# A transformer trunk on one core: two tiles of the constant pool change places, and one empty tile is put before three others

## The chip, the cores and the metric

The kernel runs on one core of one Trainium2 chip. The metric is the device time of one execution in microseconds. A core has TensorE (PE in the profile; PEld is its weight load), VectorE (DVE), ScalarE (ACT), GpSimd (POOL) and SyncE (SP, which here issues the loads). SBUF, the working memory, has 128 partitions; a tile takes the same byte range in all of them, and "offset" below means the byte within a partition at which a tile starts.

## The reference

Two layers act on 256 latent tokens and 256 context tokens of width 1024. Each layer is a half SwiGLU feed-forward, a mixer, and another half feed-forward, all modulated by a conditioning vector. The mixer of layer 0 joins bidirectional mLSTM heads and a spatial gating unit; that of layer 1 is windowed attention with rotary positions.

```python
def _modulate(h, shift, scale):
    return _rms_norm(h) * (1.0 + scale) + shift

def _swiglu(h, w_in, w_out):
    g, u = jnp.split(h @ w_in, 2, axis=-1)
    return (jax.nn.silu(g) * u) @ w_out

    for layer in range(DEPTH):
        ...
        h = h + 0.5 * mod[:, 2] * _swiglu(_modulate(h, mod[:, 0], mod[:, 1]),
                                          ffn_w_in[layer, 0], ffn_w_out[layer, 0])
        ...
        h = h + mod[:, 5] * yx
        h = h + 0.5 * mod[:, 8] * _swiglu(_modulate(h, mod[:, 6], mod[:, 7]),
                                          ffn_w_in[layer, 1], ffn_w_out[layer, 1])
    return _rms_norm(h) * final_norm
```

D_MODEL is 1024 and D_FF 2816. The context stream runs through the same layers with its own modulation vector.

## The kernel before

Activations are kept transposed: 128 features on the partitions, 8 tiles of features (kt), and 512 columns, which are the 256 context and the 256 latent tokens side by side. H is the residual stream, 8 x 512 numbers of 4 bytes per partition. The normalised and modulated activation is split into a high part NH (in the format fp32r) and a remainder NL, so that the activation is the sum of both. Weights come from memory as 1 MB tiles (raw, rawx, loaded by SP at L212), and each is split in the same way into wh (ACT, L259) and wl (DVE, L243). One product of activation and weight is then three matmuls into one PSUM bank, in the function mm3:

```python
        self.M.matmul(ps, lhsT=wh, rhs=xh, start=start, stop=False)
        self.M.matmul(ps, lhsT=wh, rhs=xl, start=False, stop=False)
        self.M.matmul(ps, lhsT=wl, rhs=xh, start=False, stop=stop)
```

These are lines 415, 416 and 417. The operand called rhs is the moving one: it is streamed through the array, 512 columns of 4 bytes for a whole tile. lhsT is the stationary one: 128 columns of a weight tile, 512 bytes per partition, loaded by a weight load before its matmul. A unit is one weight block of 128 output features; it runs mm3 for its 8 kt (6 in the last part of a down projection).

- In the up projections of a feed-forward block the moving operands are NH and NL, and wh and wl are stationary. Their results go through silu and a product into hd, which is split into HH and HL.
- In the down projections HH and HL move.
- The first four units of a block are run together by `start` and `steps` (L444) or by `split_start` (L710, in halves of 256 columns), so that the first features can be used before the last are made.
- In the mixer of layer 0 some projections are token-major (L1124 to L1126): there wh and wl move, 512 columns wide, and NH and NL are stationary. At its end the gated result is turned into the tiles Fh, Fu and Fl, which move in the output projection together with the first half of NH.
- In the last feed-forward block only the latent half is computed: NH and NL then move 258 columns, HH and HL 256.

Instructions stand in the order in which the program writes them, engine by engine. Tiles live in pools; a pool gives its tiles places one after the other in the order of first use. The pool cp (constants, made in `setup`) comes first, then the ring of raw, wh and wl, then temporaries, then pools that are opened and closed for each block. The tiles NL0 to NL7 belong to cp, behind all that `setup` makes. The pool ef, opened inside `even`, holds F.

The places in the built program, by their offset modulo 2048 (all kt slices of one tile have the same, a slice of 512 columns being 2048 bytes):

| tile | before | changed kernel |
|---|---|---|
| H, NH | 2016 | 1408 |
| NL0 to NL7 | 1408 | 1408 |
| wh, wl, raw | 1408 | 1408 |
| HH, HL | 384 | 384 |
| SS, AX, SC | 2016 | 2016 |
| Fh, Fu, Fl | 864 | 1408 |

Of the kernel before, what the change touches and what calls it, by code (L numbers as in the profile page):

```python
# [9 lines left out]
F32 = mybir.dt.float32  # L10
F32R = mybir.dt.float32r
# [9 lines left out]
KT = 8  # L21
# [125 lines left out]
class Trunk:  # L147
# [312 lines left out]
    def setup(self):  # L460
        nc, a, V, S = self.nc, self.a, self.V, self.S
        cp = self.cp
        self.SM = cp.tile([128, S_N], F32, name="SM")
        self.C = cp.tile([128, C_N], F32, name="C")
        self.H = cp.tile([128, KT, 512], F32, name="H")
        self.NH = cp.tile([128, KT, 512], F32R, tag="NH", name="NH")
        self.X = [[self.NH[:, k] for k in range(KT)], [None] * KT]
        self.A = [None] * KT
        self.SS = cp.tile([128, 512], F32, name="SS")
        self.AX = cp.tile([128, KT, 256], F32, name="AX")  # L470
        self.SC = cp.tile([128, KT, 32], F32, name="SC")
        self.ONE = cp.tile([128, 128], F32, name="ONE")
        self.NHF = cp.tile([128, 4], F32, name="NHF")
        self.IDB = cp.tile([128, 128], BF16, name="IDB")
        self.MKB = cp.tile([128, 2, 128], BF16, name="MKB")
        mods = cp.tile([128, 18, KT, 2], F32, name="mods")
        self.MOD = {(l, j): mods[:, 9 * l + j] for l in range(2) for j in range(9)}
        nc.sync.dma_start(self.SM, a["small"])
        xv = a["xt"].rearrange("(k p) t -> p k t", p=128)
        for k in range(0, KT, 2):  # L480
            nc.sync.dma_start(self.H[:, k:k + 2, :], xv[:, k:k + 2, :])
        nc.sync.dma_start(self.C, a["const"])
        self.widen("f00")
        V.memset(self.ONE, 1.0)
        V.memset(self.NHF, -0.5)
        V.memset(self.SC, 0.0)
        S.activation(self.SC[:, :, 0:2], self.SM[:, S_C:S_C + 16].rearrange("p (k s) -> p k s", s=2), AF.Silu)
        self.AB = self.SM[:, S_AB:S_AB + 144].rearrange("p (l j t) -> p l j t", l=2, j=9)
        V.tensor_scalar(self.AB[:, :, 1::3, :], self.AB[:, :, 1::3, :], 1.0, None, ALU.add)
        V.tensor_scalar(self.AB[:, :, 2::6, :], self.AB[:, :, 2::6, :], 0.5, None, ALU.mult)  # L490
        self.ID = self.C[:, C_ID:C_ID + 128]
        self.heat(HEAT[0])
        for k in range(KT):
            self.add_squares()
            self.square(k, 0, 512)
        V.tensor_copy(self.IDB, self.ID)
# [314 lines left out]
    def even(self):  # L811
# [3 lines left out]
        with self.tc.tile_pool(name="ev", bufs=1) as ep, ExitStack() as xs:  # L815
# [283 lines left out]
            def to_feature(src, t, hi, lo):  # L1099
                ps = self.bank("ptf")  # L1100
                for i in range(4):
                    M.transpose(ps[:, 128 * i:128 * i + 128], src[:, 128 * i:128 * i + 128], self.ID)
                q = slice(128 * t, 128 * t + 128)
                pv = ps.rearrange("p (k t) -> p k t", k=4)
                S.copy(hi[:, :, q], pv)
                V.tensor_tensor(lo[:, :, q], pv, hi[:, :, q].bitcast(F32), ALU.subtract)
# [66 lines left out]
            def to_u(t):  # L1173
                if not F:
                    self.drain()
                    xs.close()
                    fp = xs.enter_context(self.tc.tile_pool(name="ef", bufs=1))
                    F.extend(fp.tile([128, 4, 512], F32R, name="F" + x) for x in ("h", "u", "l"))
                to_feature(U[:, t], t, F[0], F[1])

# [3 lines left out]
            def mid(n, b, i):  # L1184
                if i == 3 and (n, b) in HAT:
                    to_h(HAT[n, b])

            self.later(*[nop] * UNOPS, *[lambda t=t: to_u(t) for t in range(4)], *[nop] * (14 - 5 - UNOPS), lambda: to_h(0))
            token_major(1536, o_evac)
            self.flush()  # L1190
# [371 lines left out]
```

## Time and profile before

| what | value |
|---|---|
| median of 3 runs | 1721.47 us (1721.23 to 1723.42) |
| the profiled execution | 1723.75 us |
| its span, first to last instruction | 1721.6 us |
| granted TensorE clock | 0.997 |
| PE busy | 1706.8 us, 9702 matmuls |
| weight loads busy | 1441.0 us |
| DVE, ACT busy | 1143.2 us, 652.8 us |
| read from memory | 245.28 MB, 143 GB/s over the span |

Busy time of PE counts a matmul from its start to its modelled end, and matmuls overlap: the mean duration in a group is longer than the time between two starts. In a row of a group, the names behind the operation are result and operands, then the stationary block (128*128), the moving shape, the count, the busy time in us, the mean of one in ns, and the idle time before with what ended it. The view by stretches gives for each stretch the busy time of each engine with the number of instructions, the granted clock and the DMA share.

### The profile page before, as it was taken

How to read it: one execution, taken by the hardware profiler on the slowest of the kernel's cores; microseconds unless marked ns; L12 is line 12 of the kernel's file. 1: busy time of each engine (PE TensorE's matmuls, PEld its weight loads, DVE VectorE, ACT ScalarE, POOL GpSimd, SP SyncE). 2: the span in 40 equal slices, each digit the busy share in tenths (PEclk: the TensorE clock that was granted, in tenths of full speed). 3: DMA queues.
4: the chain of work that ended last, by engine and by line, in shares of the span. 5: the costliest groups of instructions: out<-in, count | busy, mean ns of one | idle time of the engine just before them, and what ended most of it. 6: DMA issues, size and time to landing. Idle time of an engine off the chain costs nothing.

```text
span 1721.6 us, 23813 instructions
## 1 busy us (share of the span) xinstructions
PE 1706.8 (99%) x9702; PEld 1441.0 (84%) x9702; DVE 1143.2 (66%) x1997; ACT 652.8 (38%) x1083; POOL 24.7 (1%) x29
## 2 busy tenths in 40 slices
PE   8999999999999999999999999999999999999998
PEld 6778778779888898787787898787788897799998
DVE  5876776777877857767766367646554477576665
ACT  3422232225545444222222253222212357654444
POOL 0000000000000100000000000000000000000000
PEclk9999999999999999999999999999999999999999
DMA  9654454441211234435544134444533031165540
GB/s 352 235 179 147 171 194 144 169 153 44 98 50 49 101 121 178 185 128 193 196 147 146 38 140 183 165 161 171 196 147 123 25 123 58 50 239 188 186 156 29
DMA packets 36462, 247.87 MB, mean 144 GB/s; under 512 B 4000, under 2 KB 4256, under 8 KB 8960
## 3 DMA queue, kind: packets, MB, share of 16 engines
q1 hardware_dynamic: 35792, 244.57, 39.0%
q8 instruction: 76, 1.25, 0.3%
q0 software_dynamic: 272, 1.25, 0.2%
q10 hardware_dynamic: 288, 0.52, 0.1%
q14 instruction: 34, 0.28, 0.0%
HBM read 245.28 MB, written 1.05 MB: 143 GB/s over the span
## 4 chain that ended last, share of the span: by engine, by line
PE 96%; DVE 2%; ACT 1%; DMA 0%; issue 0%; SPq 0%; POOLq 0%; ACTq 0%; DVEq 0%
PE bank L415 25%; PE bank L417 25%; PE bank L416 25%; PE bank L710 5%; PE bank L444 4%; PE bank L1126 1%; PE bank L1125 1%; PE bank L1124 1%; PE pva L337 1%; PE pov L1314 1%; PE psc L1278 1%; PE ppt L1299 1%; PE pada L383 0%; DMA H<-xt 0%; PE pO L1006 0%; PE pB L1008 0%
## 5 line engine op out<-in xcount | busy, mean ns | idle before, releaser
L415 PE MATMUL bank<-NH,wh 128*128 128x512 f32 (+2 forms) x1416 | 519.0, 367 | 0.0
L417 PE MATMUL bank<-NH,wl 128*128 128x512 f32 (+2 forms) x1416 | 514.5, 363 | 1.2 <-DVE wl L243 1.2
L416 PE MATMUL bank<-NL,wh 128*128 128x512 f32 (+2 forms) x1384 | 499.1, 361 | 0.0
L415 PEld LDWEIGHTS bank<-NH,wh 128*128 128x128 f32 x1416 | 266.1, 188 | 48.7 <-issue 9.0
L417 PEld LDWEIGHTS bank<-NH,wl 128*128 128x128 f32 x1416 | 265.9, 188 | 47.1 <-DVE wl L243 1.7
L416 PEld LDWEIGHTS bank<-NL,wh 128*128 128x128 f32 x1384 | 260.3, 188 | 45.1
L259 ACT CAST wh<-raw 128x1024 fp32r<-128x1024 f32 (+1 forms) x207 | 212.4, 1029 | 153.6 <-PE bank L416 99.8
L415 PE MATMUL bank<-HH,wh 128*128 128x512 f32 (+1 forms) x776 | 269.8, 348 | 0.0
L416 PE MATMUL bank<-HL,wh 128*128 128x512 f32 (+1 forms) x776 | 268.4, 346 | 0.1
L417 PE MATMUL bank<-HH,wl 128*128 128x512 f32 (+1 forms) x776 | 268.4, 346 | 0.0
L243 DVE TENSOR_TENSOR wl<-raw,wh 128x1024 fp32r<-128x1024 f32 (+1 forms) x207 | 246.9, 1197 | 18.7 <-ACT wh L259 18.7
L625 DVE SCALAR_TENSOR_TENSOR H<-bank,mods,H 128x256 f32<-128x256 f32 x192 | 86.6, 480 | 174.2 <-PE bank L417 171.5
L790 ACT CAST HH<-hd 128x512 fp32r<-128x512 f32 (+1 forms) x88 | 49.9, 567 | 320.5 <-DVE hd L789 285.2
L259 ACT CAST wh<-rawx 128x1024 fp32r<-128x1024 f32 (+1 forms) x118 | 119.8, 1016 | 118.2 <-PE bank L416 102.2
L415 PEld LDWEIGHTS bank<-HH,wh 128*128 128x128 f32 x776 | 147.1, 190 | 20.3 <-issue 2.5
L416 PEld LDWEIGHTS bank<-HL,wh 128*128 128x128 f32 x776 | 147.1, 190 | 17.9 <-DVE HL L791 0.3
L417 PEld LDWEIGHTS bank<-HH,wl 128*128 128x128 f32 x776 | 147.1, 190 | 17.9
L322 DVE SCALAR_TENSOR_TENSOR va<-rawx,SC,va 128x512 f32<-128x512 f32 x228 | 159.6, 745 | 1.2
L789 DVE TENSOR_TENSOR hd<-sg,bank 128x512 f32<-128x512 f32 x66 | 45.3, 686 | 168.4 <-PE bank L417 162.9
L243 DVE TENSOR_TENSOR wl<-rawx,wh 128x1024 fp32r<-128x1024 f32 (+1 forms) x118 | 139.0, 1180 | 3.5 <-ACT wh L259 3.5
L322 DVE SCALAR_TENSOR_TENSOR va<-raw,SC,va 128x512 f32<-128x512 f32 x164 | 114.0, 745 | 0.4
L780 ACT ACTIVATE sg<-bank 128x512 f32<-128x512 f32 x66 | 39.5, 599 | 155.1 <-PE bank L417 154.6
(289 smaller groups left out, 1755.4 us busy)
## 6 DMA issues: line engine op xcount, KB each, us to landing
raw<-w SPq DMA_DIRECT2D x123, 1024.0 KB, 4.8
rawx<-w SPq DMA_DIRECT2D x91, 1024.0 KB, 4.8
rawx<-w SPq DMA_DIRECT2D x7, 768.0 KB, 4.3
raw<-w SPq DMA_DIRECT2D x6, 768.0 KB, 4.2
raw<-w SPq DMA_DIRECT2D x3, 896.0 KB, 4.5
H<-xt SPq DMA_DIRECT2D x4, 512.0 KB, 6.5
rawx<-w SPq DMA_DIRECT2D x2, 896.0 KB, 4.4
raw<-w SPq DMA_DIRECT2D x2, 512.0 KB, 8.8
```

Of the source, the lines that this page charges most:

```text
L243: self.V.tensor_tensor(lo[:, :n], src, hi[:, :n].bitcast(F32), ALU.subtract)
L259: self.S.copy(hi[:, :n], src)
L322: V.scalar_tensor_tensor(acc[:, s], src, c, acc[:, s], ALU.mult, ALU.add)
L415: self.M.matmul(ps, lhsT=wh, rhs=xh, start=start, stop=False)
L416: self.M.matmul(ps, lhsT=wh, rhs=xl, start=False, stop=False)
L417: self.M.matmul(ps, lhsT=wl, rhs=xh, start=False, stop=stop)
L444: self.M.matmul(pss[i][:, 0:hi - lo], lhsT=w[wi][:, c:c + 128], rhs=(xh, xl)[xi][kt][:, lo:hi], start=n == b == 0, stop=n == 3 and b == 5)
L625: self.V.scalar_tensor_tensor(self.H[:, m, q], ps[:, c - lo:c - lo + 256], gate[:, m, c // 256:c // 256 + 1], self.H[:, m, q], ALU.mult, A ...
L710: self.M.matmul(pss[i][:, q], lhsT=lhs, rhs=rhs, start=n == b == 0, stop=n == 3 and b == 5)
L780: S.activation(sg, pg, AF.Silu)
L789: V.tensor_tensor(hd, sg, pu, ALU.mult)
L790: S.copy(HH[:, f - fa], hd[:, 0:n])
```

## The change

In `setup` the tiles H and NH are made last instead of third and fourth. Since the tiles ahead of them are SM and C, they started at byte 18400 and 34784; behind SS, AX, SC, ONE, NHF, IDB, MKB and mods they start at 32128 and 48512. The pool keeps its size, so what follows it keeps its place. In `even` a tile of 136 numbers that nothing reads or writes is taken from the pool ef before F, which moves F by 544 bytes. The list of instructions of every engine, with what each waits for, is the same in both programs but for line numbers and running numbers in names.

```diff
@@ -462,9 +462,6 @@
         cp = self.cp
         self.SM = cp.tile([128, S_N], F32, name="SM")
         self.C = cp.tile([128, C_N], F32, name="C")
-        self.H = cp.tile([128, KT, 512], F32, name="H")
-        self.NH = cp.tile([128, KT, 512], F32R, tag="NH", name="NH")
-        self.X = [[self.NH[:, k] for k in range(KT)], [None] * KT]
         self.A = [None] * KT
         self.SS = cp.tile([128, 512], F32, name="SS")
         self.AX = cp.tile([128, KT, 256], F32, name="AX")
@@ -474,6 +471,9 @@
         self.IDB = cp.tile([128, 128], BF16, name="IDB")
         self.MKB = cp.tile([128, 2, 128], BF16, name="MKB")
         mods = cp.tile([128, 18, KT, 2], F32, name="mods")
+        self.H = cp.tile([128, KT, 512], F32, name="H")
+        self.NH = cp.tile([128, KT, 512], F32R, tag="NH", name="NH")
+        self.X = [[self.NH[:, k] for k in range(KT)], [None] * KT]
         self.MOD = {(l, j): mods[:, 9 * l + j] for l in range(2) for j in range(9)}
         nc.sync.dma_start(self.SM, a["small"])
         xv = a["xt"].rearrange("(k p) t -> p k t", p=128)
@@ -1175,6 +1175,7 @@
                     self.drain()
                     xs.close()
                     fp = xs.enter_context(self.tc.tile_pool(name="ef", bufs=1))
+                    fp.tile([128, 136], F32, name="gap")
                     F.extend(fp.tile([128, 4, 512], F32R, name="F" + x) for x in ("h", "u", "l"))
                 to_feature(U[:, t], t, F[0], F[1])
 
```

## The prediction

> **What bounds the kernel now.** I read the page first: busy time, then the chain that ended last.
>
> ```profile
> PE 1706.8 (99%) x9702; PEld 1441.0 (84%) x9702; DVE 1143.2 (66%) x1997; ACT 652.8 (38%) x1083; POOL 24.7 (1%) x29
> ...
> PE 96%; DVE 2%; ACT 1%; DMA 0%; issue 0%; SPq 0%; POOLq 0%; ACTq 0%; DVEq 0%
> ```
>
> TensorE is busy 99% of the span and makes 96% of the chain. It waits for almost nothing, so the time is the number of matmuls times their pitch, by which I mean the time from one matmul's start to the next one's. The change touches no count. The question is whether it touches the pitch. So I read the groups with shapes kept apart (columns: busy us and mean ns of one, then idle time before).
>
> ```profile
> L415 PE MATMUL bank<-NH,wh 128*128 128x512 f32 x1000 | 398.7, 399 | 0.0
> L417 PE MATMUL bank<-NH,wl 128*128 128x512 f32 x1000 | 396.9, 397 | 1.2 <-DVE wl L243 1.2
> L416 PE MATMUL bank<-NL,wh 128*128 128x512 f32 x1000 | 390.8, 391 | 0.0
> L415 PE MATMUL bank<-HH,wh 128*128 128x512 f32 x456 | 178.5, 392 | 0.0
> L417 PE MATMUL bank<-HH,wl 128*128 128x512 f32 x456 | 177.7, 390 | 0.0
> L416 PE MATMUL bank<-HL,wh 128*128 128x512 f32 x456 | 177.7, 390 | 0.0
> ```
>
> All six rows are the same instruction on the same weight buffers. Four of them take 390 to 392 ns; the two whose moving operand is NH take 397 and 399. In the built program NH starts at byte 34784 of each partition, which is 2016 modulo 2048. NL starts at 1408, HH and HL at 384, and wh and wl at 1408. A weight slice is 512 bytes, so weights start at 384, 896, 1408 or 1920. Modulo 512, then, NL, HH, HL and all weights are at 384, and NH alone is at 480.
>
> A matmul's duration holds a latency that overlaps its neighbours, so I price by pitch. I took two stretches without interruption, one of NH and NL, one of HH and HL, from the timeline of TensorE (start us, duration us), and their counts from the view by stretches.
>
> ```profile
> 1308.69 0.39 PE L416 MATMUL bank<-NL,wh 128*128 128x512 f32 x1
> ...
> 1355.82 0.40 PE L415 MATMUL bank<-HH,wh 128*128 128x512 f32 x1
> ...
> 130.51 0.39 PE L416 MATMUL bank<-HL,wh 128*128 128x512 f32 x1
> ...
> 169.75 0.40 PE L415 MATMUL bank<-NH,wh 128*128 128x512 f32 x1
> ```
>
> ```profile
> core 0: us, PE busy (x) PEld busy (x) DVE busy (x) ACT busy (x) POOL busy (x), PEclk, DMA share, GB/s
> 1308.70:1355.80 47.10, 47.10 (x204) 38.12 (x203) 14.27 (x18) 11.62 (x17) 0.00 (x0) 1.00 0.26 88
> 130.52:169.74 39.22, 39.22 (x174) 32.48 (x173) 23.94 (x37) 7.60 (x9) 0.00 (x0) 1.00 0.39 134
> 174.95:196.73 21.78, 21.78 (x95) 17.62 (x94) 16.33 (x24) 6.35 (x9) 0.00 (x0) 1.00 0.47 168
> 435.10:454.16 19.06, 19.06 (x85) 15.57 (x84) 15.00 (x42) 10.10 (x12) 0.00 (x0) 1.00 0.16 56
> 1372.18:1382.94 10.76, 10.76 (x91) 10.76 (x90) 6.21 (x13) 5.54 (x12) 0.00 (x0) 1.00 0.00 0
> 1414.55:1417.37 2.82, 2.82 (x26) 2.82 (x25) 1.50 (x2) 2.02 (x3) 0.00 (x0) 1.00 0.32 131
> ```
>
> A window also counts the matmul that was in flight at its start. So 203 NH and NL matmuls run from 1308.69 to 1355.82: 47.13 / 203 = 232.2 ns. 173 HH and HL matmuls run from 130.51 to 169.75: 39.24 / 173 = 226.8 ns. The difference is 5.4 ns on each, NL included. The clock is 1.00 in both. Other engines' traffic does not explain it: the slow stretch has DVE busy 14.27 of 47.10 us and DMA at 0.26, the fast one 23.94 of 39.22 us and 0.39. The third row is another NH stretch, with DVE at 16.33 of 21.78 us: by its 94 matmuls about 21.8 / 94 = 232 ns again. What is left as a difference is the place of the operand.
>
> **The change part by part.** No instruction is added, removed or moved, and no wait changes; I compared all five engines' lists. H and NH go from 2016 to 1408 modulo 2048 (NH to byte 48512), and F, the three tiles of the mixer's output, from 864 to 1408. SS, AX, SC, ONE, the masks and mods move, but keep their residues modulo 2048. Everything outside these two pools stays where it was.
>
> *The 512-column matmuls of L415 to L417 on NH and NL.* After the change, all their operands have the residue modulo 512 that HH, HL and the weights have now. The row nearest to them is HH's and HL's: 226.8 ns. 3000 x (232.2 - 226.8) = 16.2 us saved. The bounds: nothing saved, if placement is not the cause, and 16.2. I take 16.2, since four rows agree on the fast pitch.
>
> *The starts (L444), 512 columns.*
>
> ```profile
> L444 PE MATMUL bank<-NH,wl 128*128 128x512 f32 x48 | 14.4, 414 | 0.0
> L444 PE MATMUL bank<-NH,wh 128*128 128x512 f32 x48 | 13.6, 404 | 1.7 <-ACT NH L585 1.7
> L444 PE MATMUL bank<-NL,wh 128*128 128x512 f32 x32 | 8.7, 400 | 0.0
> ```
>
> With the 64 on F there are 192. The first 72, in the first block's start, are paced by the making of NH (the wait for ACT), and keep their time. The other 120 x 5.4 = 0.6 us saved, bounds 0 and 0.6.
>
> *Token-major matmuls (L1124 to L1126).* Here wh and wl move, and NH and NL are the stationary operand.
>
> ```profile
> L1124 PE MATMUL bank<-wh,NH 128*128 128x512 f32 x128 | 51.6, 403 | 0.0
> L1126 PE MATMUL bank<-wh,NL 128*128 128x512 f32 x128 | 50.4, 394 | 0.0
> ...
> 435.08 0.39 PE L1124 MATMUL bank<-wh,NH 128*128 128x512 f32 x1
> ...
> 454.17 0.40 PE L1126 MATMUL bank<-wh,NL 128*128 128x512 f32 x1
> ```
>
> 85 in the window less two in flight make 83: 19.09 / 83 = 230.0 ns. At 226.8, 384 x 3.2 = 1.2 us would be saved; the other bound is 0. DVE is busy 15.00 of 19.06 us there, and the 1.2 us that TensorE waited for wl (the row of L417) lie in this block, so some is given back: I take 1.0.
>
> *256 columns.* Here the aligned case is not the fast one.
>
> ```profile
> 1372.16 0.28 PE L415 MATMUL bank<-HH,wh 128*128 128x256 f32 x1
> ...
> 1382.95 0.39 PE L635 MATMUL pss<-ONE,SS 128*128 128x1 f32 x3
> ...
> 1414.53 0.28 PE L415 MATMUL bank<-NH,wh 128*128 128x256 f32 x1
> ...
> 1417.38 0.60 PE L1224 MATMUL psw<-KF,TR 128*128 128x256 f32 x2
> ...
> L415 PE MATMUL bank<-HH,wh 128*128 128x256 f32 x320 | 91.2, 285 | 0.0
> ...
> L710 PE MATMUL bank<-NH,wh 128*128 128x256 f32 x224 | 37.8, 285 | 0.0
> ...
> L415 PE MATMUL bank<-NH,wh 128*128 128x258 f32 x320 | 90.2, 282 | 0.0
> ```
>
> HH: 10.79 / 90 = 119.9 ns. NH and NL: 2.85 / 24 = 118.8 ns. Some 1150 matmuls (768 at L710, 384 at L415 to L417, F's included) could lose 1.1 ns each, 1.3 us; the other bound is 0, since L710 and HH both have 285 ns. I take 0.6 lost. The 258-column rows of the last block start 1016 bytes into a tile; NH's move to where NL's already are, so 0, between 960 x -1.1 = -1.1 and, at 5.4, +5.2 us.
>
> *H.* DVE and ACT read and write H beside matmuls, and TensorE does not wait for them. Only its load is uncovered.
>
> ```profile
> raw<-w SPq DMA_DIRECT2D x123, 1024.0 KB, 4.8
> ...
> H<-xt SPq DMA_DIRECT2D x4, 512.0 KB, 6.5
> ...
> raw<-w SPq DMA_DIRECT2D x2, 512.0 KB, 8.8
> ```
>
> By the neighbours it could gain 6.5 - 4.8 = 1.7 us or lose 8.8 - 6.5 = 2.3. I take 0, for its size and queue stay.
>
> *What a faster TensorE meets next.* Weights are prepared ahead by ACT and DVE and wait for TensorE, not the other way:
>
> ```profile
> ACT wh L259 <- PE bank L416: 202.1, 57, 4.5
> ```
>
> A pitch 2.3% shorter raises DVE's share in the NH stages from 16.33 / 21.78 = 75% to 77%. So the saved time is kept.
>
> Sum: 16.2 + 0.6 + 1.0 - 0.6 = 17.2 us saved. The profiled execution took 1723.75 us (span 1721.6), which gives 1706.6; it lies 2.3 us above the median of 1721.47, and from that median the time is **1704.3 us**.
>
> **The rivals.**
>
> *Partly: 1408 is a slow place too, only less.* The token-major rows move wh from 1408 and have 230.0 ns, not 226.8. If that is NH's price there, 3000 x 2.2 = 6.6 us are saved, nothing token-major, 0.3 at the starts, 0.6 lost: 1715.2 us. Against it: NL lies at 1408 and has 391 ns, HH's duration, between slow neighbours; and two of three token-major matmuls load weights from NH at its present place.
>
> *Nothing: the place is not the cause.* The NH stages could be slower for what surrounds them. Then only the 0.6 remains: 1722.1. For it: NL's pitch is not told apart from NH's by the 232.2. Against it: the durations do tell them apart, and the pitch is the same at 30% and 75% of DVE.
> The Trainium skill, page "SBUF — State Buffer", section "Who interferes with whom", speaks for this rival: TensorE has two independent read ports, one for the moving operand and one for weights, and waits on no other engine. Its section "Door 1: The DMA port swizzle" says that whole 16-byte lines read in a row run at full rate, and 2016 and 1408 are both multiples of 16. By these rules the change is worth 0. The trace does not agree: 397 and 399 ns against 390 to 392 for one form.
>
> *Slower: reads that start together collide.* NH would start at the offset modulo 2048 at which a weight tile starts. If moving data and the weights loaded meanwhile then hit one part of the memory, each matmul pays. The deciding point is a pitch above 232.2 ns. Priced by the only address effect that the rows show, another 5.4 ns on 3000, this is 1721.5 + 16.2 + 0.6 = 1738.3 us. Against it: NL stands in this very relation to wh and wl now and has the shortest duration of its three.
>
> **How the numbers follow.** Forecast 0.82, partly 0.08, nothing 0.06, slower 0.04. A measurement of this kernel can tell about 0.2%, 3.4 us, from no change. Forecast and partly are faster by more: 0.90. Nothing is within: 0.06. Slower: 0.04. The forecast's own range, with the unknowns of H's load, 258 columns and DVE, is 1702 to 1707. To hold 8 in 10 with a margin I reach a little below and up to the second case: 1701 to 1716.
>
> **What would show it.** Right: L415 and L417 on NH at 390 to 392 ns, like HH; a stretch of NH matmuls at 227 ns; L416 on NL unchanged; HH's rows unchanged; L1124 to L1126 nearer 227; the 256-column pitch near 120. Wrong: NH at 397 to 399 still (nothing), near 394 (partly), above 400 (collision); or NH fast and the time not, in which case the waits of L417 for wl must have grown.

## The result, and the profile after

The changed kernel takes 1706.12 us (median of 4 runs, 1705.36 to 1706.26). The kernel before, timed beside it, took 1721.5 us (1721.23 to 1723.42). The ratio is 0.9907 with a 95% interval of 0.989 to 0.9925: **15.4 us less by the medians, where 17.2 were forecast**; 1704.3 us was the predicted time. The profiled execution took 1705.36 us, its span 1703.2.

The page of the changed kernel, busy times and the chain that ended last:

```profile
PE 1689.5 (99%) x9702; PEld 1439.8 (85%) x9702; DVE 1143.2 (67%) x1997; ACT 652.9 (38%) x1083; POOL 24.7 (1%) x29
...
PE 96%; DVE 2%; ACT 1%; DMA 0%; issue 0%; SPq 0%; POOLq 0%; ACTq 0%; DVEq 0%
```

All counts are the old ones, TensorE still makes 96% of the chain, and its busy time fell from 1706.8 to 1689.5 us. The busy times of VectorE, ScalarE and GpSimd are within 0.1 us of the old ones. So the same matmuls ran at a shorter pitch. The groups with shapes kept apart (columns: busy us and mean ns of one, then idle time before) say which:

```profile
L415 PE MATMUL bank<-NH,wh 128*128 128x512 f32 x1000 | 392.9, 393 | 0.0
L417 PE MATMUL bank<-NH,wl 128*128 128x512 f32 x1000 | 389.5, 389 | 1.4 <-DVE wl L243 1.4
L416 PE MATMUL bank<-NL,wh 128*128 128x512 f32 x1000 | 389.2, 389 | 0.0
L415 PE MATMUL bank<-HH,wh 128*128 128x512 f32 x456 | 178.2, 391 | 0.0
L417 PE MATMUL bank<-HH,wl 128*128 128x512 f32 x456 | 177.4, 389 | 0.0
L416 PE MATMUL bank<-HL,wh 128*128 128x512 f32 x456 | 177.4, 389 | 0.0
...
L1124 PE MATMUL bank<-wh,NH 128*128 128x512 f32 x128 | 51.5, 402 | 0.0
L1126 PE MATMUL bank<-wh,NL 128*128 128x512 f32 x128 | 50.1, 391 | 0.0
...
L444 PE MATMUL bank<-NH,wl 128*128 128x512 f32 x48 | 14.2, 410 | 0.0
...
L444 PE MATMUL bank<-NH,wh 128*128 128x512 f32 x48 | 13.4, 401 | 1.7 <-ACT NH L585 1.7
...
L444 PE MATMUL bank<-NL,wh 128*128 128x512 f32 x32 | 8.7, 400 | 0.0
```

The two NH rows, 399 and 397 ns before, stand at 393 and 389. NL and the HH and HL rows differ by at most 2 ns from their old values. For the pitch I take the prediction's stretches of 203 NH and NL matmuls and of 83 token-major ones, and another stretch of 173 HH and HL matmuls, in a later block. From the timeline of TensorE (start us, duration us), the first and last start of the first and the third stretch:

```profile
427.90 0.40 PE L1124 MATMUL bank<-wh,NH 128*128 128x512 f32 x1
...
446.74 0.39 PE L1126 MATMUL bank<-wh,NL 128*128 128x512 f32 x1
...
1291.79 0.39 PE L416 MATMUL bank<-NL,wh 128*128 128x512 f32 x1
...
1337.83 0.39 PE L415 MATMUL bank<-HH,wh 128*128 128x512 f32 x1
```

From the view by stretches, with the columns of the prediction's:

```profile
427.91:446.73 18.82, 18.82 (x85) 15.58 (x84) 14.79 (x41) 10.10 (x12) 0.00 (x0) 1.00 0.16 57
861.93:901.15 39.22, 39.22 (x174) 32.46 (x173) 23.94 (x37) 7.61 (x9) 0.00 (x0) 1.00 0.36 126
1291.80:1337.82 46.02, 46.02 (x204) 38.09 (x203) 14.27 (x18) 11.62 (x17) 0.00 (x0) 1.00 0.26 93
```

NH and NL: 46.04 / 203 = **226.8 ns**, where it was 232.2. HH and HL keep 226.8 (39.24 / 173; their first start is at 861.92, their last at 901.16). Token-major: 18.84 / 83 = 227.0 ns, where it was 230.0. DVE, ACT and the DMA share in the NH stretch are what they were (14.27, 11.62, 0.26).

### The profile page after: what moved, and what is told of

It reads as the page before. It is cut to its first block, busy times and chain, and to the rows that moved or that the text cites. A ratio compares the mean times of both kernels' runs of the same rounds, so it can differ in the third digit from the quotient of the medians.

```text
span 1703.2 us, 23813 instructions
## 1 busy us (share of the span) xinstructions
PE 1689.5 (99%) x9702; PEld 1439.8 (85%) x9702; DVE 1143.2 (67%) x1997; ACT 652.9 (38%) x1083; POOL 24.7 (1%) x29
## 4 chain that ended last, share of the span: by engine, by line
PE 96%; DVE 2%; ACT 1%; DMA 0%; issue 0%; SPq 0%; POOLq 0%; ACTq 0%; DVEq 0%
PE bank L415 25%; PE bank L417 25%; PE bank L416 25%; PE bank L710 5%; PE bank L444 4%; PE bank L1124 1%; PE bank L1126 1%; PE bank L1125 1%; PE pva L337 1%; PE pov L1315 1%; PE psc L1279 1%; PE ppt L1300 1%; PE pada L383 0%; PE pO L1006 0%; DMA H<-xt 0%; PE pB L1008 0%
## 5 line engine op out<-in xcount | busy, mean ns | idle before, releaser
L415 PE MATMUL bank<-NH,wh 128*128 128x512 f32 (+2 forms) x1416 | 513.2, 362 | 0.0
L417 PE MATMUL bank<-NH,wl 128*128 128x512 f32 (+2 forms) x1416 | 506.7, 358 | 1.4 <-DVE wl L243 1.4
L416 PE MATMUL bank<-NL,wh 128*128 128x512 f32 (+2 forms) x1384 | 497.3, 359 | 0.0
L415 PEld LDWEIGHTS bank<-NH,wh 128*128 128x128 f32 x1416 | 266.2, 188 | 47.1 <-issue 9.0
L417 PEld LDWEIGHTS bank<-NH,wl 128*128 128x128 f32 x1416 | 266.1, 188 | 41.3 <-DVE wl L243 1.8
L416 PEld LDWEIGHTS bank<-NL,wh 128*128 128x128 f32 x1384 | 260.2, 188 | 38.3
L415 PE MATMUL bank<-HH,wh 128*128 128x512 f32 (+1 forms) x776 | 269.3, 347 | 0.0
L416 PE MATMUL bank<-HL,wh 128*128 128x512 f32 (+1 forms) x776 | 268.1, 345 | 0.1
L417 PE MATMUL bank<-HH,wl 128*128 128x512 f32 (+1 forms) x776 | 268.0, 345 | 0.0
L415 PEld LDWEIGHTS bank<-HH,wh 128*128 128x128 f32 x776 | 146.9, 189 | 20.2 <-issue 2.5
L416 PEld LDWEIGHTS bank<-HL,wh 128*128 128x128 f32 x776 | 147.0, 189 | 18.0 <-DVE HL L791 0.3
L417 PEld LDWEIGHTS bank<-HH,wl 128*128 128x128 f32 x776 | 147.0, 189 | 17.9
```

## The experiments

The result leaves two readings of "place". **R, relative**: a matmul is slow when its moving operand and its weights start at different offsets within some small block of bytes. **A, absolute**: it is slow when the moving operand itself starts at a bad offset. Before, NH was at 480 modulo 512 and NL, HH, HL and all weights at 384, so the two can't be told apart by the change. Below, "at 384" and "at 480" mean modulo 512, and "x off" means x bytes further on than its partner in this sense.

The pitch in every run is read from the same 203-matmul stretch of NH and NL. A window of it lies inside the first and the last start by 0.02 us in all (0.03 in the run with the weights moved), and it counts one more matmul, in flight at its start. So the pitch is (window + 0.02) / 203.

### Which of the moved tiles matters

NH alone is moved; H and F stay:

```diff
         self.H = cp.tile([128, KT, 512], F32, name="H")
-        self.NH = cp.tile([128, KT, 512], F32R, tag="NH", name="NH")
-        self.X = [[self.NH[:, k] for k in range(KT)], [None] * KT]
...
         mods = cp.tile([128, 18, KT, 2], F32, name="mods")
+        self.NH = cp.tile([128, KT, 512], F32R, tag="NH", name="NH")
+        self.X = [[self.NH[:, k] for k in range(KT)], [None] * KT]
```

> NH alone goes to byte 48512 (1408 modulo 2048); H stays at 18400 (2016) and F at 864. If the gain is the pitch of matmuls on NH, both theories of its cause below give nearly all of it: 512-column NH stretches at 227 ns instead of 232, token-major near 227, F's few matmuls unchanged: 1706 to 1707 us. If the load of H or the engines' accesses to H matter, at least 1 us of the gain is missing: 1707.5 or more.

And the rest of the change without it; NH moves by 16384 bytes, so it keeps 2016 modulo 2048:

```diff
-        self.H = cp.tile([128, KT, 512], F32, name="H")
         self.NH = cp.tile([128, KT, 512], F32R, tag="NH", name="NH")
...
         mods = cp.tile([128, 18, KT, 2], F32, name="mods")
+        self.H = cp.tile([128, KT, 512], F32, name="H")
...
                     fp = xs.enter_context(self.tc.tile_pool(name="ef", bufs=1))
+                    fp.tile([128, 136], F32, name="gap")
```

> The rest of the change: H goes to 48512 (1408) and F to 1408; NH is at 18400, which is 2016 modulo 2048 as before. By the pitch on NH: 512-column NH stretches still at 232 ns, the time within 1 us of before (F's 64 matmuls of 512 columns give 0.3 us). If H's place matters: 1720 us or less.

The NH stretch with NH alone moved:

```profile
1293.52:1339.54 46.02, 46.02 (x204) 38.11 (x203) 14.28 (x18) 11.63 (x17) 0.00 (x0) 1.00 0.25 92
```

The NH stretch with H and F alone moved:

```profile
1307.31:1354.42 47.11, 47.11 (x204) 38.09 (x203) 14.28 (x18) 11.62 (x17) 0.00 (x0) 1.00 0.24 88
```

NH alone has the whole gain: 46.04 / 203 = 226.8 ns and 1706.39 us (1704.52 to 1706.99), a ratio of 0.9899 (0.9885 to 0.9914). H and F alone have none: 47.13 / 203 = 232.2 ns and 1722.58 us, 0.9998 (0.9989 to 1.0007). The second also shows that NH's byte address as such is not what counts: 16384 bytes lower, the pitch is the same to 0.1 ns.

### Relative or absolute

Here NH stays at 480, and the other operands of these matmuls come to 480 too. A gap of 96 bytes behind `mods` shifts NL, raw, wh, wl, HH and HL:

```diff
         mods = cp.tile([128, 18, KT, 2], F32, name="mods")
+        cp.tile([128, 24], F32, name="gap")
...
-            t1 = self.tp.tile([128, 512], F32, tag="ada1", name="ada1", bufs=2)
+            t1 = self.tp.tile([128, 256], F32, tag="ada1", name="ada1", bufs=2)
```

> NH and H stay where they were (2016); an empty tile of 96 bytes behind mods moves NL, raw, wh, wl, HH and HL by 96, so that all of them are at 480 modulo 512, like NH. (To make room, a temporary of the ada part is 256 columns wide instead of 512, which is all of it that is used.) Theory R, that the moving and the stationary operand must start at the same offset modulo some power of two: all 512-column stretches at 227 ns, NH's and HH's, and a time of about 1706 us. Theory A, that the moving operand must itself start on a line of 128 bytes, whatever the weights do: NL, HH and HL turn slow as NH is. Two of three operands cost 16.2 us over 3000 matmuls now, 8.1 ns each; 1000 on NL and 1368 on HH and HL more make 19 us: about 1740 us.

And the mirror image, on the changed kernel: NH and NL stay at 384, and the gap ahead of the weight tiles brings wh, wl and, behind them, HH and HL to 480 (the second edit of the last diff is in it too):

```diff
         src = self.raw[g][:, c:c + n]
+        if i == 0:
+            self.ring.tile([128, 24], F32, name="rgap", bufs=1)
         hi = self.ring.tile([128, 1024], F32R, tag="wh", name="wh")
```

> The changed kernel with an empty tile of 96 bytes between raw and wh: NH and NL at 384 modulo 512, wh and wl at 480, and HH and HL, which lie behind them, at 480. (The same temporary is 256 columns wide.) Theory R: NH and NL are off against the weights, HH and HL are not. NH and NL stretches at 232 ns or more (all three matmuls of a triple are off now: by 8.1 ns each, up to 235), HH stretches at 227: 1722 to 1731 us. Theory A: NH and NL stretches at 227 ns, HH stretches at 232 to 235: 1706 + 1368 x 8.1 = 1717 us.

NH, NL, HH, HL and the weights at 480 alike, the HH stretch and the NH stretch:

```profile
862.81:902.03 39.22, 39.22 (x174) 32.46 (x173) 23.95 (x37) 7.61 (x9) 0.00 (x0) 1.00 0.35 126
1292.66:1338.69 46.03, 46.03 (x204) 38.11 (x203) 14.28 (x18) 11.63 (x17) 0.00 (x0) 1.00 0.26 92
```

NH and NL at 384, weights, HH and HL at 480:

```profile
874.62:913.84 39.22, 39.22 (x174) 32.47 (x173) 23.95 (x37) 7.60 (x9) 0.00 (x0) 1.00 0.35 125
1311.60:1359.13 47.53, 47.53 (x204) 38.22 (x203) 14.28 (x18) 11.61 (x17) 0.00 (x0) 1.00 0.24 86
```

With all of them at 480 the kernel is as fast as the changed one: 226.8 ns and 1705.87 us, 0.9897 (0.9882 to 0.9911), though not one operand was brought to a rounder place. With NH and NL where the change puts them and the weights 96 bytes further on, the gain is gone: 47.56 / 203 = 234.3 ns and 1725.16 us, 1.0015 (1.0005 to 1.0025). Its HH stretch, both operands at 480, is fast. **R stands, A falls.** Nor is it the distance from NH to NL, which is 0 in this slow run. That the last run is slower than the kernel before fits this too: all three matmuls of a product are now off, where before it was two of three (NL was not). Per matmul that is off: 234.3 - 226.8 = 7.5 ns here, and 3 x 5.4 / 2 = 8.1 ns before.

### How large the block is, and how the cost depends on the distance

NH was put 32, 64, 128 and 256 bytes off by moving it ahead of other tiles of the same pool, and HH and HL of the last block, which move 256 columns, were put off by as much, with an empty tile. The run at 32:

```diff
+        self.IDB = cp.tile([128, 128], BF16, name="IDB")
+        self.NHF = cp.tile([128, 4], F32, name="NHF")
+        self.NH = cp.tile([128, KT, 512], F32R, tag="NH", name="NH")
+        self.X = [[self.NH[:, k] for k in range(KT)], [None] * KT]
         self.SM = cp.tile([128, S_N], F32, name="SM")
...
         with self.tc.tile_pool(name=f"ffn{l}{i}", bufs=1) as fp:
+            if c0:
+                fp.tile([128, 8], F32, name="hgap")
```

(The lines that made these tiles further down are gone.) At 128 `mods` stands ahead of NH in place of NHF, and the empty tile has 32 numbers; at 256 nothing stands ahead of NH, and it has 64; at 64 the empty tile has 16, and there are two more around NH and the 256-column `ada1` again.

> How fine is the rule? NH alone is moved, to 416 modulo 512: 32 bytes past the weights' 384. In the last feed-forward block HH and HL, which move 256 columns there, are also put 32 bytes past them. If any difference counts: 512-column NH stretches at 232 ns, the time about that of before; if only the same line of 64 or 128 bytes counts, 227. For 256 columns, by the 118.8 ns of NH at 96 bytes against HH's 119.9: 117 to 119 ns.

> NH alone, and HH and HL of the last block, 64 bytes past the weights' residue. If the rule is one of lines of 64 bytes: NH stretches at 227 ns and about 1706 us, HH at 120 ns. If of 128 or more: 232 ns and about 1722 us, HH at 117 to 119.

> NH alone, and HH and HL of the last block, 128 bytes past the weights' residue. If the rule is one of lines of 128 bytes or less: NH stretches at 227 ns and about 1706 us, HH at 120 ns. If of 256 or 512: 232 ns, about 1722 us.

> NH alone, and HH and HL of the last block, 256 bytes past the weights' residue. If the rule is one of 256 bytes or less: NH stretches at 227 ns and about 1706 us, HH at 120 ns. If it is modulo 512, which is the length of a weight slice: 232 ns, about 1722 us.

In each of the four fences below the first row is the NH stretch, the second a stretch of 192 HH and HL matmuls of 256 columns in the last block (two more in flight). 32 off:

```profile
1303.68:1350.57 46.89, 46.89 (x204) 38.12 (x203) 14.28 (x18) 11.62 (x17) 0.00 (x0) 1.00 0.25 89
1562.42:1584.80 22.38, 22.38 (x194) 22.38 (x193) 13.75 (x19) 8.74 (x9) 0.00 (x0) 1.00 0.55 189
```

64 off:

```profile
1308.81:1356.15 47.34, 47.34 (x204) 38.05 (x203) 14.28 (x18) 11.62 (x17) 0.00 (x0) 1.00 0.25 88
1568.12:1590.71 22.59, 22.59 (x194) 22.59 (x193) 13.76 (x19) 8.71 (x9) 0.00 (x0) 1.00 0.52 187
```

128 off:

```profile
1297.05:1343.49 46.44, 46.44 (x204) 38.07 (x203) 14.28 (x18) 11.60 (x17) 0.00 (x0) 1.00 0.26 91
1555.61:1578.63 23.02, 23.02 (x194) 23.02 (x193) 13.76 (x19) 8.73 (x9) 0.00 (x0) 1.00 0.54 185
```

256 off:

```profile
1292.63:1338.65 46.02, 46.02 (x204) 38.09 (x203) 14.28 (x18) 11.63 (x17) 0.00 (x0) 1.00 0.26 92
1550.86:1573.87 23.01, 23.01 (x194) 23.01 (x193) 13.76 (x19) 8.70 (x9) 0.00 (x0) 1.00 0.55 185
```

| NH off the weights by (bytes) | pitch, 512 columns (ns) | time (us) | pitch of HH and HL, 256 columns, as far off (ns) |
|---|---|---|---|
| 0 (changed kernel) | 226.8 | 1706.12 | 120.0 |
| 32 | 231.1 | 1716.51 | 116.7 |
| 64 | 233.3 | 1722.89 | 117.8 |
| 96 (before) | 232.2 | 1721.5 | not tried |
| 128 | 228.9 | 1711.12 | 120.0 |
| 256 | 226.8 | 1705.98 | 120.0 |

At 512 columns two matmuls of three are off in these rows (NL is not moved), at 256 columns all three. The four new rows are one execution each (the kernel before took 1720.88 us beside them), so their times carry about 0.1%; the pitches are steadier. The expectation for 128 knew only 227 and 232, and the measured 228.9 lies between. Two things follow. 256 off is as good as 0, and HH and HL, which lie 1024 off the weights in the kernel before and in the changed one, are fast as well. Since 128 off still costs 2.1 ns, the block that fits is 256 bytes: the offset need not be the same modulo 2048, as the change has it. And for 256 columns the sign is the other way round: 32 or 64 off is faster than 0 by 3.3 or 2.2 ns.

The pitch is the mean over a product's three matmuls. Taken one by one over the whole trace, the intervals from the start of L416 on NL, whose operands are 0 off each other in all these runs, have 230.9 ns at 32 and 232.2 at 64, nearly as much as those of L415 and L417, but 228.5 at 96 and 225.9 at 128. An interval ends with the start of the next matmul, so the cost can't be laid on the matmul whose own operands are apart alone.

### Can the other sign be used

The changed kernel again, to repeat it and to get its 256- and 258-column stretches in one trace:

> The changed kernel once more, as the base for the next two on the same chip: 1706 us.

With HH and HL of the last block, and OH and OL of layer 1's output projection, put 32 off:

```diff
         with self.tc.tile_pool(name=f"ffn{l}{i}", bufs=1) as fp:
+            if c0:
+                fp.tile([128, 8], F32, name="hgap")
...
             VT = op.tile([128, 4, 256], F32, name="VT")
+            op.tile([128, 8], F32, name="ogap")
             OH = op.tile([128, KT, 256], F32R, name="OH")
             OL = op.tile([128, KT, 256], F32R, name="OL")
+            op.tile([128, 56], F32, name="ogap2")
```

> The changed kernel, with the operands that only ever move 256 columns put 32 bytes past the weights' residue: HH and HL of the last block, OH and OL of the attention's output projection. If the 116.7 ns measured for HH at 32 bytes is a rule for all 256-column matmuls: 512 x (119.96 - 116.7) = 1.7 us and 192 x 3.3 = 0.6 us saved, 2.3 us, below what one comparison can tell from none, but the stretches must stand at 116.7 ns. If it is particular to that stage, OH's and OL's stay at 120.

And with NH's and NL's 258 columns of the last block besides, kept in columns 200 to 457 in place of 254 to 511, which makes them 32 off in place of 248 (the same as 8 short of the next block; 0 off is not tried):

```diff
-        x, y = slice(256, 512), slice(254, 256)
+        x, xx, y = slice(256, 512), slice(202, 458), slice(200, 202)
...
-            c1 = c0 and c0 - 2
+            c1 = 200 if c0 else 0
+            c2 = 458 if c0 else 512
...
-                self.unit(u, ps[:, 0:512 - c1], c1, 512)
+                self.unit(u, ps[:, 0:c2 - c1], c1, c2)
```

> As the kernel before this one, and in the last block the 258 columns of NH and NL that move there are kept in columns 200 to 457 of their tiles instead of 254 to 511, so that they too start 32 bytes past the weights' residue modulo 256 (800 bytes into a tile at 1408). If the rule holds for 258 columns: 119.1 to 120.0 ns become about 117.5 ns (116.7 and two columns more), some 1050 x 2.2 = 2.3 us on top, together 4.6 us below the changed kernel, about 1701.5 us. If not: equal to the kernel before this one.

The changed kernel again: 96 matmuls of OH and OL, 287 of NH and NL with 258 columns, 192 of HH and HL, 384 of NH and NL with 258 columns.

```profile
1490.15:1501.65 11.50, 11.50 (x98) 11.50 (x97) 10.27 (x27) 9.12 (x19) 0.00 (x0) 1.00 0.48 178
1514.59:1549.02 34.43, 34.43 (x289) 34.43 (x288) 25.12 (x54) 19.54 (x29) 0.00 (x0) 1.00 0.56 204
1549.04:1572.05 23.01, 23.01 (x194) 23.01 (x193) 13.76 (x19) 8.69 (x9) 0.00 (x0) 1.00 0.56 185
1572.07:1617.77 45.70, 45.70 (x386) 45.70 (x385) 31.71 (x61) 22.17 (x31) 0.00 (x0) 1.00 0.52 184
```

HH, HL, OH and OL 32 off, the first, third and fourth of these stretches, and a second one of HH and HL behind them:

```profile
1492.43:1503.61 11.18, 11.18 (x98) 11.18 (x97) 9.96 (x27) 8.80 (x19) 0.00 (x0) 1.00 0.45 174
1550.68:1573.07 22.39, 22.39 (x194) 22.39 (x193) 13.77 (x19) 8.71 (x9) 0.00 (x0) 1.00 0.55 189
1573.09:1618.79 45.70, 45.70 (x386) 45.70 (x385) 31.71 (x61) 22.19 (x31) 0.00 (x0) 1.00 0.52 185
1618.81:1641.41 22.60, 22.60 (x194) 22.60 (x193) 13.77 (x19) 8.74 (x9) 0.00 (x0) 1.00 0.52 182
```

The 258 columns 32 off too, the same stretches of HH and HL and of 384:

```profile
1550.08:1572.67 22.59, 22.59 (x194) 22.59 (x193) 13.77 (x19) 8.73 (x9) 0.00 (x0) 1.00 0.53 187
1572.69:1618.75 46.06, 46.06 (x386) 46.06 (x385) 31.71 (x61) 22.19 (x31) 0.00 (x0) 1.00 0.51 183
```

The 384 matmuls of 258 columns in the run with the weights moved by 96 bytes (above), where they are 152 off:

```profile
1593.62:1638.84 45.22, 45.22 (x386) 45.22 (x385) 31.70 (x61) 22.17 (x31) 0.00 (x0) 1.00 0.53 185
```

OH and OL went from 120.0 to 116.7 ns (11.52 and 11.20 us for 96), HH and HL from 120.0 to 116.7 (23.03 and 22.41 for 192) in one stretch and 117.8 (22.62) in the other. In the second run the same stretch of HH and HL, as far off, has 117.8 (22.61): at this width the distance does not fix the pitch alone, and 116.7 at 32 and 117.8 at 64 are not shown to differ by the distance. The 258 columns went the wrong way, from 119.1 to 120.0 ns (45.72 and 46.08 for 384): that expectation missed. At this width, too, the distance is not all, since the changed kernel has 120.0 in its first stretch (34.45 / 287) and 119.1 in the long one, both 248 off. But it matters: 152 off it is 117.8 ns (45.24 / 384). By the medians nothing here is told from the changed kernel, which took 1704.31 us this time (ratio 0.9895, 0.9881 to 0.991): 1703.42 us (0.989, 0.9875 to 0.9904) and 1704.79 us (0.9895, 0.9878 to 0.9911).

### Where the scatter of the times is

A gain of 2 us is lost in medians that differ by 1.8 us for one kernel (1706.12 and 1704.31). But the traces say where the scatter is. Their summary for L415 in the first 60 us shows count, duration (minimum, median, maximum in ns), and the first and last start in us; the span stands above it, and for the first two kernels the view of the first 25 us. Kernel before:

```profile
core 0 of [0], span 1721.6 us
...
0.00:25.00 25.00, 20.25 (x137) 17.61 (x138) 10.11 (x28) 9.21 (x16) 1.21 (x5) 0.86 0.93 362
...
L415 PE MATMUL bank<-NH,wh x5: 390/394/397, 57.0 to 59.8; 128*128 128x512 f32 x5
```

The changed kernel:

```profile
core 0 of [0], span 1703.2 us
...
0.00:25.00 25.00, 21.44 (x157) 18.01 (x158) 12.11 (x33) 9.86 (x17) 1.21 (x5) 0.93 0.94 365
...
L415 PE MATMUL bank<-NH,wh x8: 389/389/389, 54.8 to 59.6; 128*128 128x512 f32 x8
```

The changed kernel again:

```profile
core 0 of [0], span 1702.2 us
...
L415 PE MATMUL bank<-NH,wh x10: 389/389/389, 53.8 to 59.9; 128*128 128x512 f32 x10
```

H and F alone moved:

```profile
core 0 of [0], span 1720.2 us
...
L415 PE MATMUL bank<-NH,wh x7: 389/394/396, 55.6 to 59.8; 128*128 128x512 f32 x7
```

HH, HL, OH and OL 32 off:

```profile
core 0 of [0], span 1702.4 us
...
L415 PE MATMUL bank<-NH,wh x6: 389/389/389, 56.3 to 59.7; 128*128 128x512 f32 x6
```

The first L415 matmul starts at 53.8 to 57.0 us, and at 54.8 and 53.8 for one and the same kernel. From there to the end it is 1721.6 - 57.0 = 1664.6 us for the kernel before and 1720.2 - 55.6 = 1664.6 with H and F alone moved; 1703.2 - 54.8 = 1648.4 and 1702.2 - 53.8 = 1648.4 for the changed kernel twice. This part repeats to about 0.1 us, so it can be compared between single traces: **the change saves 16.2 us in it**, and the 32 bytes on HH, HL, OH and OL another 2.3 (1702.4 - 56.3 = 1646.1). With the 258 columns 32 off too, 1.2 of that are lost again (1702.6 - 55.3 = 1647.3). What varies is the part ahead of it, in which the first tiles are loaded and the first block's NH is made. One thing that goes with it is the granted clock of the first 25 us: it is 0.93 in the two traces of the changed kernel, 0.86 in the other three. Over the 13 traces of this case, those at 0.93 start L415 at 53.8 to 55.1 us and those at 0.86 at 55.3 to 57.0; what sets the rest of the scatter is not shown. The version with the 32 bytes on HH, HL, OH and OL is thus the fastest by its one trace, by 0.14%, and the comparison of medians can't confirm it.

## Why the prediction was right, point by point

*What bounds the kernel.* Right. Nothing but the pitch changed, and the saved time was kept: TensorE's idle time before L417 went from 1.2 to 1.4 us.

*The 512-column matmuls of L415 to L417: 16.2 us forecast.* Right in mechanism, a little high in size. The pitch of the stretch fell to HH's, from 232.2 to 226.8, as priced. Means are 233.3, 228.5 and 234.8 ns for L415, L416 and L417 before, and 227.2, 227.0 and 227.0 after (starts from the timeline, intervals across other work left out): 6.1, 1.5 and 7.8 ns less. All 3000 intervals, those across other work included, went from 703.8 to 688.8 us: 15.0 us, since such intervals did not shrink and the undisturbed stretch was taken for all. Measuring also mends a reading of the prediction, 5.4 ns on NL too: at 96 off the intervals of NL itself were hardly slow (228.5), and the 5.4 ns stood almost wholly in those of the two matmuls that move NH. The price on all three came out nearly right since it was taken from the triple as a whole. L415 and L417 on NH ended at 393 and 389 ns, not quite in the band of 390 to 392 that was named as the sign.

*Starts: 0.6 forecast.* About 0.5, by the intervals from the first L415 on, 0.3 of it on F and 0.2 on NH and NL. The L444 rows went from 404, 414 and 400 ns to 401, 410 and 400.

*Token-major: 1.0 forecast.* 384 x (230.0 - 227.0) = 1.2 us by the stretch, 0.8 by the intervals of all of them. Here the weights move and NH is stationary, and the distance counts there as well. The reserve of 0.2 us made for DVE was thus 0.2 too small; the wait of L417 for wl, in this block, grew by 0.2 us (1.2 to 1.4).

*256 columns: -0.6 forecast.* -0.7: L710 lost 0.3 us, F 0.3 and NH and NL of L415 to L417 0.1. The sign was right, and the runs at other distances bear it out: at 0 off HH and HL have 120.0 ns, at 32 off 116.7 to 117.8. Why the sign turns is open.

*258 columns: 0 forecast, between -1.1 and +5.2.* About +0.6: L417 fell from 121.3 to 119.6 ns, L416 from 120.0 to 119.3, and L415 rose from 118.7 to 119.2. The argument, that NH goes where NL is, was right; that this costs nothing and gains nothing was not quite.

*H: 0 forecast, between -1.7 and +2.3.* Nothing. Its load landed in 6.0 us in place of 6.5, and moving H and F alone gives a ratio of 0.9998 (0.9989 to 1.0007).

*The sum.* From the first L415 on, 16.2 us were saved, so the forecast of 17.2 was 1.0 too much: the term of 16.2 measures 15.0, three others were 0.1 to 0.2 too good, the 258 columns gave 0.6 that was not counted, and HH's intervals 0.2. That the forecast sum lies so near is in part that the last two made up for the first. The spans differ by 18.4 us, since the profiled execution before came to its first L415 2.2 us later than the one after. The medians differ by 15.4; that is 0.8 off 16.2, less than the scatter ahead of the first L415 (3.2 us between these traces).

*The rivals.* "Partly" falls: with NH, NL and the weights at 1408, the pitch is 226.8, not 230.0, and 1408 is neither good nor bad by itself. "Slower" falls: the same offset modulo 2048 costs nothing, and no distance tried is faster at 512 columns. "Nothing" falls, and with it what was drawn from the Trainium skill, page "SBUF — State Buffer", section "Who interferes with whom": two independent read ports would make the distance between the operands indifferent. In these runs the distance alone moves the pitch from 226.8 to 234.3 ns, at equal clock and with equal work beside it. Whether two reads meet in one port is not shown.

*What was argued beyond what was known.* The prediction named the residue modulo 512 and let the reader think of a good and a bad place for NH. The runs say that there is none at 512 columns: the distance to the weights counts, and modulo 256 bytes fits every distance tried.

## What to carry to other kernels

Where TensorE is busy 99% of the span, look for rows of one instruction form with different mean durations, and compare the start offsets of both their operands. For 512-column fp32r matmuls with a weight load each, give the moving and the stationary operand the same offset modulo 256 bytes; an empty tile of a few numbers does it, and here it was worth 0.9%. Don't carry the rule to other widths without a run (at 256 columns 0 off was the slower place), and read a gain of 0.1% from a stretch that repeats, not from medians that hold the scatter of the start.

## What the hardware showed that was not expected

- The distance between moving and stationary operand changes the pitch at 512 columns: 226.8 ns at 0 and 256, 231.1 at 32, 233.3 at 64, 232.2 at 96, 228.9 at 128 bytes, with two matmuls of three off. The absolute place does not matter (226.8 with NH, NL, HH, HL and the weights all at 480).
- At 256 columns 32 off is faster, 116.7 to 117.8 against 120.0 ns at 0; at 258 columns 32 off has 120.0, 248 off 119.1 or 120.0, 152 off 117.8.
- From the first L415 to the end, 1650 us of work repeat to about 0.1 us between the traces of one kernel; their scatter lies in the first 57 us, and there it goes with the granted clock, 0.93 or 0.86 over the first 25 us.

What stays open: why the distance costs anything. The runs don't tell whether a moving stream is disturbed by the load of its own weights or by that of the next matmul's, nor why 256 and 258 columns differ from 512. At 512 columns it is shown that the two operands' distance is what counts; by what means is not.
